# Column sums of the modulation by a product with ones, on a decoder block of one core

## The chip, the cores and the metric

The kernel runs on one core of one Trainium2 chip. The metric is the device time of one execution in microseconds (us), lower is better. TensorE (PE) multiplies, VectorE (DVE) does the elementwise work, ScalarE (ACT) activations and copies, GpSimd (POOL) and SyncE (SP) issue most of the DMAs.

## The reference

One decoder block over 512 tokens of width 2048, all in f32. A condition vector c gives six modulation vectors of 2048 each, `mod = silu(c) @ w_ada + b_ada`: shift, scale and gate of the first half, then of the second.

```
shift1, scale1, gate1, shift2, scale2, gate2 = split(mod, 6)
h = rms_norm(x, norm1_w) * (1 + scale1) + shift1
proj = h @ w_in                      # 7168 columns: attention q, k, v and recurrence q, f, i, g
attn = rms_norm(dilated_attention(q, k, v), attn_out_norm_w)
hg = rms_norm(hgrn2(...), hg_norm_w) * silu(g)
x = x + gate1 * (concat(attn, hg) @ w_out)
h2 = rms_norm(x, norm2_w) * (1 + scale2) + shift2
x = x + gate2 * (square(relu(h2 @ w_ff1)) @ w_ff2)
```

## The kernel before

**Products.** Every f32 operand of the big products is split into a rounded part (hi) and a rest (lo), and each product is three: hi hi, hi lo, lo hi. `_split` makes the two parts of the weights (whi on ScalarE, L39; wlo on VectorE, L40), with four buffers of each. So one block k (128 rows of the input width) of a group of four column blocks is 12 products of 512 moving columns, in `ch_mm` and `tok_mm` (L198 to L200, L206 to L208).

**The modulation.** It is a matrix-vector product with 100 MB of weights and runs on VectorE (`gemv`): each 128 rows of w_ada are multiplied by one number per partition and added into one of two accumulators `acc` (L127, L129). What is left is the sum over the 128 partitions, as one number per column, in a column layout: `to_cols`. It turns each 128 columns of the accumulators with a transpose on TensorE (L149), and ScalarE sums each row of the result with an accumulating copy (L152, an ACTIVATE and a read of the accumulator). For 512 columns the two accumulators are first added on VectorE (L143), so there are four transposes; for 256 columns both are turned, which is four too. Then VectorE adds the bias (L167) and, for a scale, makes (1 + scale) times norm weight (L169). `mod_cols` does this for one block of columns of one kind (kind 0 is shift1, 1 scale1, 2 gate1, 3 shift2, 4 scale2, 5 gate2), and `mod_rows` for a whole gate.

**The first stage.** The projection starts before all of the modulation is there. `first_groups` multiplies columns 4096 to 4607 and 3072 to 3327 of w_in with the normalised input scaled by scale1, block k by block k. Ahead of each pair of blocks `scale_block` finishes the sum of the 256 columns of scale1 that it needs; `scaled` then scales xnT (L332), rounds it to hi (L333) and takes the rest lo (L334). Shift1 is added later: for these columns `shift_through` multiplies shift1 itself by w_in, as a second matrix-vector product, and for all others `shifted` remakes hi and lo (L337 to L339). The second `first_groups` call takes the next 512 + 256 columns, with `shift_block` making shift1 in four blocks of 512 meanwhile.

**Order.** A scheduler places the instructions of this first part from its own estimate of their times; each engine then runs its queue strictly in order. From the projection of columns 5120 on (`hv0`) TensorE's order is the written one: the rest of the modulation (the list `later`: gate1, then scale2 and shift2 by turns, then gate2) is cut into steps by `yield`, and `project` takes 1.85 of them for each block k (2.0 in `hv0`). `tc.issue_after(ins)` places what is traced under it behind `ins` on its engine's queue.

Of the kernel before, what the change touches and what calls it, by code (L numbers as in the profile page):

```python
# [11 lines left out]
AF = mybir.ActivationFunctionType  # L12
ALU = mybir.AluOpType
AX = mybir.AxisListType

P = 128
D = 2048
S = 512
NK = D // P
# [25 lines left out]
def hybrid_block(ctx, tc, x, c, positions, norm1_w, w_ada, b_ada, w_in, q_norm_w, k_norm_w,  # L45
# [3 lines left out]
    pe, dve, act, pool = nc.tensor, nc.vector, nc.scalar, nc.gpsimd  # L49
# [18 lines left out]
    def bank(name, tag="bg"):  # L68
        return ps.tile([P, 512], F32, name=name, tag=tag)


    ident = const.tile([P, P], F32, name="ident")
    make_identity(nc, ident)
    mhalf = const.tile([P, 32], F32, name="mhalf")
    pool.memset(mhalf, -0.5)

    crow = ca.tile([P, P], F32, name="crow", tag="rows")
    nc.sync.dma_start(crow[0:NK], c[0].rearrange("(r p) -> r p", p=P))
# [4 lines left out]
    n1c = const.tile([P, NK], F32, name="n1c")  # L83
    dve.tensor_copy(n1c, ps_c[:, NK:2 * NK])
    bcol = const.tile([P, 96], F32, name="bcol")
    dve.tensor_copy(bcol, ps_c[:, 2 * NK:P])
    sc = const.tile([P, NK], F32, name="sc")
    sig_ready = act.activation(sc, ps_c[:, 0:NK], AF.Sigmoid)
    sc_ready = dve.tensor_tensor(sc, ps_c[:, 0:NK], sc, op=ALU.mult)
# [10 lines left out]
    n2c, aoc, hgc, posc = cols[:, 0:16], cols[:, 16:24], cols[:, 40:41], cols[:, 44:48]  # L100
# [15 lines left out]
    def gemv(view, vec, col0, n=512, early=False):  # L116

        accs = [(work("acc") if early else gv.tile([P, 512], F32, name="acc"))[:, 0:n] for _ in range(2)]
        nk = 512 // n
        for k0 in range(0, NK, nk):  # L120
            raw = spare.pop(0) if early and spare else slot("araw") if early else gv.tile([P, 512], F32, name="araw", bufs=4)
            raw = raw.rearrange("p (k n) -> p k n", n=n)
            nc.sync.dma_start(raw, view[:, k0:k0 + nk, col0:col0 + n])
            for k in range(k0, k0 + nk):
                acc = accs[k % 2]
                if k < 2:
                    dve.tensor_scalar(acc, raw[:, k - k0], vec[:, k:k + 1], None, op0=ALU.mult)  # L127
                else:
                    dve.scalar_tensor_tensor(acc, raw[:, k - k0], vec[:, k:k + 1], acc, op0=ALU.mult, op1=ALU.add)  # L129
            yield  # L130
        gemv.acc = accs

# [2 lines left out]
            pass  # L135
        return gemv.acc

    def to_cols(accs, dst):

        nb = accs[0].shape[1] // P  # L140
        parts = 1 if nb == 4 else 2
        if parts == 1:
            dve.tensor_tensor(accs[0], accs[0], accs[1], op=ALU.add)  # L143
        yield
        pc = bank("pc")
        for j in range(nb):
            for u in range(parts):
                c = (j * parts + u) * P
                pe.transpose(pc[:, c:c + P], accs[u][:, j * P:(j + 1) * P], ident)  # L149
        for j in range(nb):  # L150
            c = pc[:, j * parts * P:(j + 1) * parts * P]
            act.activation(c, c, AF.Copy, accum_out=dst[:, j:j + 1])  # L152

    g1c = const.tile([P, NK], F32, name="g1c")
    s1c = const.tile([P, NK], F32, name="s1c")
# [4 lines left out]
    def mod_cols(kind, b, dst, nw, n=512, early=False):  # L160

        for _ in gemv(ada_v, sc, kind * D + b * n, n, early):
            yield
        nb = n // P
        d = dst[:, b * nb:(b + 1) * nb]
        yield from to_cols(gemv.acc, d)
        dve.tensor_tensor(d, d, bcol[:, kind * NK + b * nb:kind * NK + (b + 1) * nb], op=ALU.add)  # L167
        if nw is not None:
            mod_cols.last = dve.scalar_tensor_tensor(d, d, 1.0, nw[:, b * nb:(b + 1) * nb], op0=ALU.add, op1=ALU.mult)  # L169
        yield  # L170

    def mod_rows(kind, dst):
# [53 lines left out]
    def slot(name, dt=F32):  # L226
        return io.tile([P, 512], dt, name=name, tag="io")

    def work(name, dt=F32):
        return wk.tile([P, 512], dt, name=name, tag="wk")  # L230

    def pair(i):

        return [hp.tile([P, S], F32R, name=f"{c}{i}", tag=f"{c}{i}") for c in ("hi", "lo")]
# [7 lines left out]
    hhi, hlo, spare = [], [], []  # L242
# [11 lines left out]
    for q in range(4):  # L254
        for ti in range(NT):
            jk = work("jk")
            with tc.issue_after(sc_ready.ins), tc.issue_after(sig_ready.ins):
                if q == 3 and ti % 2:
                    dve.tensor_tensor_reduce(jk, xs[ti][q], xs[ti][q], op0=ALU.mult, op1=ALU.add, scale=1.0, scalar=0.0,
                                             accum_out=ssx[:, ti, q:q + 1])  # L260
# [9 lines left out]
    xnT = []  # L270
# [36 lines left out]

    def shift_start(k0):
        if k0 == 14:
            for _ in range(12):  # L310
                bg_step()

    shift_done, behind = set(), []

# [14 lines left out]
    def scaled(k):  # L329
        for l, t in zip((hhi, hlo), pair(k)):  # L330
            l.append(t)
        act.activation(xnT[k], xnT[k], AF.Copy, scale=g1c[:, k:k + 1])  # L332
        act.copy(hhi[k], xnT[k])  # L333
        dve.tensor_tensor(hlo[k], xnT[k], hhi[k].bitcast(F32), op=ALU.subtract)  # L334

    def shifted(k):
# [6 lines left out]
    def bg_step():  # L343

        while bgw:
            try:
                return next(bgw[0])
            except StopIteration:
                bgw.pop(0)
# [198 lines left out]
    def forget(hd, src, f, bias=0.0):  # L548
        act.activation(f, src, AF.Sigmoid, bias=bias)
        dve.tensor_scalar(f, f, omlb[:, hd:hd + 1], lb[:, hd:hd + 1], op0=ALU.mult, op1=ALU.add)  # L550
# [182 lines left out]
    def keep(banks, name, scale=1.0):  # L733
        ts = []
        for b in banks:
            t = slot(name)
            act.activation(t, b, AF.Copy, scale=scale)
            ts.append(t)
        return ts

    def shift_through(col0):

        yield from gemv(win_v, s1c, col0, early=col0 < 4096 + 512)
        col = sm.tile([P, 8], F32, name="scol", bufs=2)
        yield from to_cols(gemv.acc, col[:, 0:4])
        for h in range(4):
            if col0 == 3072:
                dve.tensor_scalar(col[:, 4 + h:5 + h], col[:, h:h + 1], QS, None, op0=ALU.mult)
                sg = wk.tile([P, 512], F32, name="sg", tag="ev", bufs=2)
                act.activation(sg, hq0[h], AF.Sigmoid, scale=1.0 / QS, bias=col[:, h:h + 1])  # L750
                dve.scalar_tensor_tensor(hq0[h], hq0[h], col[:, 4 + h:5 + h], sg, op0=ALU.add, op1=ALU.mult)
            else:
                f, hd = ((f0, h), (f1, 4 + h))[(col0 - 4096) // 512]
                forget(hd, f[h], f[h], col[:, h:h + 1])
        yield

    bgw += [shift_through(4096), shift_through(3072)]
    bt, bc = first_groups(4096, 3072, scale_block, shift_start)
    f0 = keep(bt, "f")
    hq0 = keep(bc, "gq", QS)  # L760
    with tc.issue_after(mod_cols.last.ins):
        posf = ca.tile([NT, P], F32, name="posf")
        dve.tensor_copy(posf, posi)
        ps_v = bank("ps_v")
        pe.transpose(ps_v[:, 0:P], rows, ident)
        pe.transpose(ps_v[:, P:P + NT], posf, ident[0:NT, 0:NT])
        dve.tensor_copy(cols[:, 0:41], ps_v[:, 0:41])
        dve.tensor_copy(posc, ps_v[:, P:P + NT])


# [23 lines left out]
        for e in (20, 10, 0):  # L794
            u = float(2.0 ** e)
            k = rp[:, (4 + len(turns)) * 64:(5 + len(turns)) * 64]
# [26 lines left out]
    hq0 += keep(bc, "gq", QS)  # L823

    later.insert(0, shift_through(4096 + 512))

    ordered = ctx.enter_context(ExitStack())
# [552 lines left out]
```

## Time and profile before

| what | value |
|---|---|
| median of 3 runs | 2307.28 us (2306.57 to 2311.78) |
| profiled execution | 2306.17 us, its span 2304.4 us |
| mean granted TensorE clock | 0.994 |
| TensorE busy | 2230.5 us (97%) |
| VectorE busy | 1825.9 us (79%) |
| ScalarE busy | 1103.0 us (48%) |

The span is the recorded part of an execution, some 2 us shorter than its time. A busy time counts a stretch in which at least one instruction of the engine runs; products overlap, so the mean length of one product is longer than the distance from one to the next, and distances are taken from starts. A row of a timeline gives start, length, engine, line, operation, out<-in, shapes and count, and in brackets the idle time ahead and what ended it. A row of a group gives the count, then busy time and mean ns of one, then the idle time ahead. A row of waits gives the total, how many times, and the longest. In the chain of waits a row is start, length and what ran.

### The profile page before, as it was taken

To read this page: it belongs to the slowest core of one execution; us is meant where nothing else is said; L and a number is where in the kernel's file an instruction comes from. 1 tells how busy PE (TensorE), PEld (TensorE's weight loads), DVE (VectorE), ACT (ScalarE), POOL (GpSimd) and SP (SyncE) were. 2 spreads that over 40 slices of the span, in tenths; PEclk is the share of its full clock that TensorE was granted. 3 is DMA by queue.
4 is the path that set the end of the run, shared out by engine and by line. 5 is a ranking of instruction groups with operands and counts; after the bars stand their busy time and mean duration, and the time that the engine had idled before them with its cause. 6 is when DMAs were issued, how large, how long until landed. Compare 5 with 4: busy or idle time off the path is not lost.

```text
span 2304.4 us, 33163 instructions
## 1 busy us (share of the span) xinstructions
PE 2230.5 (97%) x11769; PEld 1829.2 (79%) x11769; DVE 1825.9 (79%) x2773; ACT 1103.0 (48%) x1958; POOL 458.1 (20%) x668
## 2 busy tenths in 40 slices
PE   4999999999999999999999999999998999999999
PEld 3787877888778888888887888888887888888887
DVE  6899777677776565669767988988895789967878
ACT  5555434433344553457644555565563333344332
POOL 1000022000230000001332323323232222222221
PEclk9999999999999999999999999999999999999999
DMA  9798455556545256746999799889889987999784
GB/s 327 249 337 314 123 176 156 176 162 215 178 149 182 74 186 218 259 132 220 366 382 382 252 341 355 301 297 380 310 295 369 339 288 262 364 336 335 277 302 165
DMA packets 264695, 606.71 MB, mean 263 GB/s; under 512 B 23284, under 2 KB 44032, under 8 KB 264528
## 3 DMA queue, kind: packets, MB, share of 16 engines
q1 hardware_dynamic: 186800, 332.54, 42.8%
q0 software_dynamic: 72832, 262.60, 31.1%
q10 hardware_dynamic: 4896, 9.44, 1.2%
q8 instruction: 93, 1.52, 0.3%
q14 instruction: 74, 0.61, 0.1%
HBM read 522.68 MB, written 81.81 MB: 262 GB/s over the span
## 4 chain that ended last, share of the span: by engine, by line
PE 56%; DMA 16%; DVE 14%; issue 10%; POOL 2%; ACT 1%; SPq 0%; DVEq 0%; POOLq 0%; ACTq 0%
PE f L1160 9%; PE f L1161 9%; PE f L1159 9%; DMA araw<-in_w_ada_dram 7%; PE prj L198 4%; PE prj L200 4%; PE prj L199 4%; DMA f_lod<-fs 3%; DVE acc L129 3%; PE f L208 2%; PE f L206 2%; PE f L207 2%; DVE vlo L1146 2%; DVE wlo L40 2%; PE prj L206 2%
## 5 line engine op out<-in xcount | busy, mean ns | idle before, releaser
L1145 ACT CAST vhi<-raw 128x1024 fp32r<-128x1024 f32 x392 | 412.8, 1055 | 547.1 <-PE f L1161 434.3
L1146 DVE TENSOR_TENSOR vlo<-raw,vhi 128x1024 fp32r<-128x1024 f32 x392 | 477.4, 1225 | 154.3 <-ACT vhi L1145 153.5
L1159 PE MATMUL f<-vhi,Fh 128*128 128x512 f32 x1376 | 537.6, 391 | 8.3 <-DMA Fh<-h_hid 3.6
L1160 PE MATMUL f<-vlo,Fh 128*128 128x512 f32 x1376 | 538.1, 391 | 3.0 <-DVE vlo L1146 3.0
L1161 PE MATMUL f<-vhi,Fl 128*128 128x512 f32 x1376 | 537.2, 390 | 2.1 <-DMA Fl<-f_lod 1.3
L39 ACT CAST whi<-wraw 128x512 fp32r<-128x512 f32 (+1 forms) x368 | 219.8, 601 | 449.3 <-PE prj L200 323.7
L198 PE MATMUL prj<-whi,hi 128*128 128x512 f32 x896 | 365.0, 407 | 1.3 <-ACT gg L698 1.3
L200 PE MATMUL prj<-whi,lo 128*128 128x512 f32 x896 | 351.5, 392 | 0.0
L199 PE MATMUL prj<-wlo,hi 128*128 128x512 f32 x896 | 350.8, 391 | 0.0
L40 DVE TENSOR_TENSOR wlo<-wraw,whi 128x512 fp32r<-128x512 f32 (+1 forms) x368 | 245.1, 670 | 111.7 <-ACT whi L39 107.1
L129 DVE SCALAR_TENSOR_TENSOR acc<-araw,sc,acc 128x512 f32<-128x512 f32 (+1 forms) x392 | 253.9, 678 | 98.5 <-DMA araw<-in_w_ada_dram 97.2
L1159 PEld LDWEIGHTS f<-vhi,Fh 128*128 128x128 f32 x1376 | 259.0, 188 | 63.3 <-issue 7.1
L1160 PEld LDWEIGHTS f<-vlo,Fh 128*128 128x128 f32 x1376 | 259.0, 188 | 61.7 <-DVE vlo L1146 8.3
L1161 PEld LDWEIGHTS f<-vhi,Fl 128*128 128x128 f32 x1376 | 259.1, 188 | 56.7 <-DMA Fl<-f_lod 1.8
L1129 DVE TENSOR_TENSOR raw<-raw,raw 128x1024 f32<-128x1024 f32 x224 | 269.5, 1223 | 1.8 <-DMA raw<-in_w_ff_dram 1.5
L198 PEld LDWEIGHTS prj<-whi,hi 128*128 128x128 f32 x896 | 169.4, 189 | 36.5 <-ACT gg L698 1.6
L200 PEld LDWEIGHTS prj<-whi,lo 128*128 128x128 f32 x896 | 168.9, 188 | 36.8
L199 PEld LDWEIGHTS prj<-wlo,hi 128*128 128x128 f32 x896 | 169.6, 189 | 32.4 <-DVE wlo L40 0.4
L1097 POOL DMA_DIRECT2D Fh<-f_hid x112 | 80.9, 722 | 428.3 <-PE f L1161 414.8
L208 PE MATMUL f<-hi,wlo 128*128 128x512 f32 x256 | 99.8, 390 | 0.6 <-DVE wlo L40 0.6
L206 PE MATMUL f<-hi,whi 128*128 128x512 f32 x256 | 100.2, 391 | 0.0
L207 PE MATMUL f<-lo,whi 128*128 128x512 f32 x256 | 99.6, 389 | 0.0
(306 smaller groups left out, 2956.9 us busy)
## 6 DMA issues: line engine op xcount, KB each, us to landing
raw<-in_w_ff_dram SPq DMA_DIRECT2D x224, 512.0 KB, 10.0
araw<-in_w_ada_dram SPq DMA_DIRECT2D x384, 256.0 KB, 4.3
Fh<-f_hid POOLq DMA_DIRECT2D x112, 512.0 KB, 6.5
Fl<-f_lod POOLq DMA_DIRECT2D x112, 512.0 KB, 7.4
wraw<-in_w_in_dram SPq DMA_DIRECT2D x104, 512.0 KB, 4.1
Fh<-h_hid POOLq DMA_DIRECT2D x60, 512.0 KB, 6.8
Fl<-h_lod POOLq DMA_DIRECT2D x60, 512.0 KB, 8.3
f_hid<-part POOLq DMA_DIRECT2D x48, 512.0 KB, 8.1
```

The costliest lines, as they stand in the source:

```text
L39: nc.scalar.copy(hi, src)
L40: (eng or nc.vector).tensor_tensor(lo, src, hi.bitcast(F32), op=ALU.subtract)
L129: dve.scalar_tensor_tensor(acc, raw[:, k - k0], vec[:, k:k + 1], acc, op0=ALU.mult, op1=ALU.add)
L198: pe.matmul(banks[ti], lhsT=hi[:, ts], rhs=whi, start=first, stop=False)
L199: pe.matmul(banks[ti], lhsT=hi[:, ts], rhs=wlo, start=False, stop=False)
L200: pe.matmul(banks[ti], lhsT=lo[:, ts], rhs=whi, start=False, stop=last)
L1129: dve.tensor_tensor(dst, a, b, op=ALU.subtract)
L1145: act.copy(hi, src)
L1146: split_done.append(dve.tensor_tensor(lo, src, hi.bitcast(F32), op=ALU.subtract))
L1159: pe.matmul(banks[t], lhsT=fh[u][:, a, ts], rhs=whi[:, a], start=first, stop=False)
L1160: pe.matmul(banks[t], lhsT=fh[u][:, a, ts], rhs=wlo[:, a], start=False, stop=False)
L1161: pe.matmul(banks[t], lhsT=fl[u][:, a, ts], rhs=whi[:, a], start=False, stop=end)
```

## The change

The transposes and the accumulating copies go. `col_sums` multiplies each 128 columns of an accumulator, as the weights of a product, by one column of ones; the two accumulators of a sum are added up in PSUM. For 512 columns that is eight products with one moving column, for 256 four. The sum of the two accumulators on VectorE (L143) goes too. For a scale, ScalarE then makes each column of (1 + scale) times norm weight straight from PSUM with an Identity activation, with the norm weight as scale and a bias that `scale_bias` has once made for all columns, (1 + b) times norm weight. For the other kinds one VectorE addition of the bias reads PSUM.

Three edits of order come with it. `scaled` makes the rounded part hi first, and the scaled xnT after it. The twelve first steps of the shift sums are placed behind the last instruction of the scale sums (`shift_start`). And the sums of `shift_through` are issued five steps behind their matrix-vector product, not one.

```diff
-    pool.memset(mhalf, -0.5)
+    pool.memset(mhalf[:, 0:16], -0.5)
+    pool.memset(mhalf[:, 16:32], 1.0)
+    ones = mhalf[:, 16:17]
...
+    def scale_bias(kind, nw):
+        b = bcol[:, kind * NK:(kind + 1) * NK]
+        return dve.scalar_tensor_tensor(b, b, 1.0, nw, op0=ALU.add, op1=ALU.mult)
+    scale_bias(1, n1c)
...
-    def to_cols(accs, dst):
-        nb = accs[0].shape[1] // P
-        parts = 1 if nb == 4 else 2
-        if parts == 1:
-            dve.tensor_tensor(accs[0], accs[0], accs[1], op=ALU.add)
-        yield
-        pc = bank("pc")
-        for j in range(nb):
-            for u in range(parts):
-                c = (j * parts + u) * P
-                pe.transpose(pc[:, c:c + P], accs[u][:, j * P:(j + 1) * P], ident)
-        for j in range(nb):
-            c = pc[:, j * parts * P:(j + 1) * parts * P]
-            act.activation(c, c, AF.Copy, accum_out=dst[:, j:j + 1])
+    def col_sums(accs, lag=1, tag="bg"):
+        for _ in range(lag):
+            yield
+        pc = bank("pc", tag=tag)
+        for j in range(accs[0].shape[1] // P):
+            for u in range(2):
+                pe.matmul(pc[:, j:j + 1], lhsT=accs[u][:, j * P:(j + 1) * P], rhs=ones, start=u == 0, stop=u == 1)
+        return pc
+    def to_cols(accs, dst, lag=1, tag="bg"):
+        pc = yield from col_sums(accs, lag, tag)
+        act.copy(dst, pc[:, 0:dst.shape[1]])
...
-        yield from to_cols(gemv.acc, d)
-        dve.tensor_tensor(d, d, bcol[...], op=ALU.add)
-        if nw is not None:
-            mod_cols.last = dve.scalar_tensor_tensor(d, d, 1.0, nw[...], op0=ALU.add, op1=ALU.mult)
+        pc = yield from col_sums(gemv.acc)
+        if nw is None:
+            dve.tensor_tensor(dst[...], pc[:, 0:nb], bcol[...], op=ALU.add)
+        else:
+            for j in range(nb):
+                k = b * nb + j
+                mod_cols.last = act.activation(dst[:, k:k + 1], pc[:, j:j + 1], AF.Identity, scale=nw[:, k:k + 1],
+                                               bias=bcol[:, kind * NK + k:kind * NK + k + 1])
+            mod_cols.last_dve = gemv.last
...
     def shift_start(k0):
         if k0 == 14:
-            for _ in range(12):
-                bg_step()
+            with tc.issue_after(mod_cols.last_dve.ins):
+                for _ in range(12):
+                    bg_step()
...
+        act.activation(hhi[k], xnT[k], AF.Copy, scale=g1c[:, k:k + 1])
         act.activation(xnT[k], xnT[k], AF.Copy, scale=g1c[:, k:k + 1])
-        act.copy(hhi[k], xnT[k])
...
-        yield from to_cols(gemv.acc, col[:, 0:4])
+        yield from to_cols(gemv.acc, col[:, 0:4], 5)
```

The lines of the changed kernel are numbered anew: L129 is L138 there, L149 is L155, L332 and L333 are L347 and L346, L198 to L200 are L211 to L213, L206 to L208 are L219 to L221.

ScalarE's queue at the first two blocks k, before:

```order
L282 COPY xnT<-ptx 128x512 x2
L332 ACTIVATE xnT<-xnT,g1c 128x512
L282 COPY xnT<-ptx 128x512
L332 ACTIVATE xnT<-xnT,g1c 128x512
L282 COPY xnT<-ptx 128x512
L39 CAST whi<-wraw 128x512 x2
L333 CAST hi_473<-xnT 128x512
```

And now:

```order
L295 COPY xnT<-ptx 128x512 x2
L346 ACTIVATE hi_471<-xnT,g1c 128x512
L295 COPY xnT<-ptx 128x512
L346 ACTIVATE hi_476<-xnT,g1c 128x512
L295 COPY xnT<-ptx 128x512
L39 CAST whi<-wraw 128x512 x2
L347 ACTIVATE xnT<-xnT,g1c 128x512
```

The rounded parts of both blocks stand ahead of the two weight casts, where the scaling of xnT stood.

VectorE's queue at the last three scale sums (128x256 are scale sums, 128x512 shift sums), before:

```order
L129 SCALAR_TENSOR_TENSOR acc<-araw,sc,acc 128x512
L129 SCALAR_TENSOR_TENSOR acc<-araw,sc,acc 128x256
L129 SCALAR_TENSOR_TENSOR acc<-araw,sc,acc 128x512
L169 SCALAR_TENSOR_TENSOR g1c<-g1c,n1c 128x2
L40 TENSOR_TENSOR wlo<-wraw,whi 128x256
L129 SCALAR_TENSOR_TENSOR acc<-araw,sc,acc 128x256
L167 TENSOR_TENSOR g1c<-g1c,bcol 128x2
L129 SCALAR_TENSOR_TENSOR acc<-araw,sc,acc 128x512
L129 SCALAR_TENSOR_TENSOR acc<-araw,sc,acc 128x256
```

And now:

```order
L138 SCALAR_TENSOR_TENSOR acc<-araw,sc,acc 128x256 x3
L348 TENSOR_TENSOR lo_999<-xnT,hi_998 128x512
L348 TENSOR_TENSOR lo_1004<-xnT,hi_1003 128x512
L40 TENSOR_TENSOR wlo<-wraw,whi 128x256 x2
L138 SCALAR_TENSOR_TENSOR acc<-araw,sc,acc 128x256 x6
L136 TENSOR_SCALAR acc<-araw,sc 128x512 x2
```

The first shift sum (L136 on 128x512) stands behind the last of the scale sums, and the g1c instructions are gone from this queue.

TensorE's queue at the sums of the fourth block of shift1, before (in the products of `hv0`, its 13th product group):

```order
L199 MATMUL prj<-wlo,hi_579 128x512
L200 MATMUL prj<-whi,lo_580 128x512
L149 MATMUL pc<-ident,acc 128x128 x4
L198 MATMUL prj<-whi,hi_579 128x512
L199 MATMUL prj<-wlo,hi_579 128x512
```

And now (in the second `first_groups` call, ahead of its block k = 14):

```order
L220 MATMUL prc<-lo_1111,whi 128x512
L221 MATMUL prc<-hi_1110,wlo 128x512
L155 MATMUL pc<-mhalf,acc 128x1 x8
L219 MATMUL prj<-hi_1171,whi 128x512
L220 MATMUL prj<-lo_1172,whi 128x512
```

Eight products with the ones (a column of mhalf) stand where four transposes stood, and 75 products earlier in the queue.

More of the change, by code (lines that the diff above doesn't have):

```diff
@@ L128, in gemv @@
                 else:
-                    dve.scalar_tensor_tensor(acc, raw[:, k - k0], vec[:, k:k + 1], acc, op0=ALU.mult, op1=ALU.add)
+                    gemv.last = dve.scalar_tensor_tensor(acc, raw[:, k - k0], vec[:, k:k + 1], acc, op0=ALU.mult,
+                                                         op1=ALU.add)
             yield
@@ L164, in mod_cols @@
         nb = n // P
-        d = dst[:, b * nb:(b + 1) * nb]
-        yield from to_cols(gemv.acc, d)
-        dve.tensor_tensor(d, d, bcol[:, kind * NK + b * nb:kind * NK + (b + 1) * nb], op=ALU.add)
-        if nw is not None:
-            mod_cols.last = dve.scalar_tensor_tensor(d, d, 1.0, nw[:, b * nb:(b + 1) * nb], op0=ALU.add, op1=ALU.mult)
+        pc = yield from col_sums(gemv.acc)
+        if nw is None:
+            dve.tensor_tensor(dst[:, b * nb:(b + 1) * nb], pc[:, 0:nb],
+                              bcol[:, kind * NK + b * nb:kind * NK + (b + 1) * nb], op=ALU.add)
+        else:
[4 more added lines that the diff above has]
+            mod_cols.last_dve = gemv.last
         yield
@@ L760, in hybrid_block @@
     hq0 = keep(bc, "gq", QS)
-    with tc.issue_after(mod_cols.last.ins):
+    with tc.issue_after(mod_cols.last.ins), tc.issue_after(mod_cols.last_dve.ins):
         posf = ca.tile([NT, P], F32, name="posf")
@@ L767, in hybrid_block @@
         dve.tensor_copy(cols[:, 0:41], ps_v[:, 0:41])
+        scale_bias(4, n2c)
         dve.tensor_copy(posc, ps_v[:, P:P + NT])
```

## The prediction

> **What bounds the kernel now.** I read the page's busy times first, then busy time by stretch, then TensorE's waits, then the timelines around each wait.
>
> ```profile
> span 2304.4 us, 33163 instructions
> PE 2230.5 (97%) x11769; PEld 1829.2 (79%) x11769; DVE 1825.9 (79%) x2773; ACT 1103.0 (48%) x1958; POOL 458.1 (20%) x668
> 0.00:240.00 240.00, 199.44 (x877) 162.27 (x878) 206.32 (x454) 127.20 (x289) 14.93 (x33) 0.96 0.88 300
> 240.00:1070.00 830.00, 814.80 (x5470) 663.67 (x5469) 601.71 (x1258) 387.80 (x1006) 82.64 (x127) 1.00 0.54 170
> 1070.00:2304.00 1234.00, 1216.24 (x5426) 1003.28 (x5424) 1017.84 (x1063) 587.96 (x665) 360.50 (x508) 1.00 0.87 319
> ```
>
> The first column after the bounds is the stretch, then come TensorE's busy time, its weight loads, VectorE, ScalarE, GpSimd, clock, DMA share and GB/s. TensorE bounds everything. It idles 40.6 us in the first 240 us, only 15.2 us in the 830 us after (the rest of the modulation's work lies there), and 17.8 us in the last 1234 us, which the change doesn't touch. So time is to be won ahead of 240 us, and what is added to TensorE behind it is paid nearly in full. The 40.6 us:
>
> ```profile
> PE ptx L280 <- ACT xs L274: 12.7, 1, 12.7
> PE prj L206 <- ACT hi L333: 6.9, 4, 4.1
> PE pc L149 <- DVE acc L143: 4.9, 1, 4.9
> ```
>
> The 12.7 us and what precedes them wait for x, which the change leaves alone. The other two rows are its targets. Their places, and the clock behind them:
>
> ```profile
> 37.06 1.19 PE L206 MATMUL prj<-hi,whi 128*128 128x512 f32 x4 [0.68 <-ACT hi L333]
> 52.75 2.02 PE L206 MATMUL prj<-hi,whi 128*128 128x512 f32 x4 [1.97 <-ACT hi L333]
> 58.58 1.07 PE L206 MATMUL prj<-hi,whi 128*128 128x512 f32 x4
> 94.46 2.07 PE L206 MATMUL prj<-hi,whi 128*128 128x512 f32 x4 [4.05 <-ACT hi L333]
> 101.66 1.07 PE L206 MATMUL prj<-hi,whi 128*128 128x512 f32 x4
> 105.75 0.27 PE L149 MATMUL pc<-ident,acc 128*128 128x128 f32 x1
> 214.98 1.12 PE L149 MATMUL pc<-ident,acc 128*128 128x128 f32 x4 [4.86 <-DVE acc L143]
> 215.75 0.78 PE L198 MATMUL prj<-whi,hi 128*128 128x512 f32 x1
> 220.59 0.40 PE L198 MATMUL prj<-whi,hi 128*128 128x512 f32 x1
> ```
>
> One row block k takes 18 products (4 + 2 column blocks, three each). Undisturbed that is 101.66 to 105.75, 4.09 us or 0.227 us a product. Behind the wait at 52.75 the same 18 take 5.83 us (to 58.58), behind the one at 94.46 7.20 us (to 101.66), and behind 214.98 twelve products take 4.84 us instead of 2.73. So each wait costs a second time, through the slow clock after it: 1.7, 3.1 and 2.1 us.
>
> **The change part by part.** First, the way from a finished scale sum to TensorE. For the block that stopped TensorE at 94.46:
>
> ```profile
> 85.32 0.49 PE L149 MATMUL pc<-ident,acc 128*128 128x128 f32 x3
> 85.84 0.37 ACT L152 ACTIVATE pc<-pc 128x256 f32<-128x256 f32 x1 [0.62 <-PE pc L149]
> 88.84 0.17 DVE L167 TENSOR_TENSOR g1c<-g1c,bcol 128x2 f32<-128x2 f32 x1
> 92.36 0.17 DVE L169 SCALAR_TENSOR_TENSOR g1c<-g1c,n1c 128x2 f32<-128x2 f32 x1
> 92.57 1.33 ACT L332 ACTIVATE xnT<-xnT,g1c 128x512 f32<-128x512 f32 x2 [1.14 <-DVE g1c L169]
> 93.81 1.12 ACT L333 CAST hi<-xnT 128x512 fp32r<-128x512 f32 x2
> 60.00:80.00 20.00, 19.78 (x92) 16.10 (x91) 20.00 (x53) 10.70 (x25) 0.00 (x0) 1.00 1.09 354
> 80.00:100.00 20.00, 15.65 (x60) 11.73 (x59) 20.00 (x48) 9.09 (x21) 0.00 (x0) 0.84 0.77 262
> 100.00:120.00 20.00, 20.00 (x90) 16.26 (x89) 13.56 (x46) 10.10 (x21) 0.00 (x0) 0.98 0.29 80
> ```
>
> From the product at 85.32 to the rounded part at 93.81 pass 8.5 us, though the rows between them hold 2.0 us of work: the two tiny VectorE instructions stand in the queue of an engine busy 20.00 of 20 us. After the change ScalarE does it alone: two instructions on one column each, at most the 0.37 us of the row at 85.84, then at once the rounded part, whose scaled xnT comes behind it. That is about 1.5 us and no VectorE. The wait at 94.46 and the one at 52.75 should go. ScalarE has room (about 10 of 20 us), so its added work costs nothing; if it had none, 0.7 us a block would show. The first rounded part moves ahead of two weight casts, which gives most of the 0.68 us at 37.06. Of 6.9 us of waits I take 4.9 as gained and leave 2.0, since the sums themselves come at the pace of a full VectorE; with 1.7 + 3.1 of clock that is **-9.7 us**.
>
> The shift sums queued behind, the second edit, help here:
>
> ```profile
> L129 DVE SCALAR_TENSOR_TENSOR acc<-araw,sc,acc 128x512 f32<-128x512 f32 x10 | 7.7, 769 | 0.0
> L143 DVE TENSOR_TENSOR acc<-acc 128x512 f32<-128x512 f32 x7 | 5.0, 715 | 0.0
> ```
>
> Ten shift sums, 7.7 us, stood between the last scale sums. Now they wait for the last of them; behind them are queued later shift sums, and TensorE's first shift product waits for those. VectorE's idle 6.4 us at 100 to 120 us take most of the ten, so no term. The DMAs that feed them keep their place in SP's queue, behind the same w_in loads. The L143 sums go, 5.0 us of VectorE up to 235 us; that is under a busy TensorE, and serves as slack.
>
> At 214.98 TensorE waited for a sum of the f columns' shift, whose product is now issued four steps later (two blocks k in the projection, 5.4 us of products), and the 4.86 + 2.1 us go: **-7.0 us**.
>
> Now what TensorE pays. A transpose is one record; an f32 product is two. The ten products of one head in L498 are 20 records, each with its own weight load; so the 8 products of 512 columns are 16 records where 4 stood, and the 4 of a scale block 8. No row shows a product with one moving column. The nearest rows, from the chain (first two), from the groups, and the timeline (last):
>
> ```profile
> 440.26 2.23 PE po L498 x20
> 1700.86 1.75 PE pt L1189 x16
> L498 PEld LDWEIGHTS po<-av,p_sb 128*128 128x128 f32 x160 | 19.1, 192 | 0.6
> L651 PEld LDWEIGHTS pC<-z 128*64 128x64 f32 x64 | 4.3, 137 | 2.9 <-issue 1.1 <-DVE z L598 0.4 <-DVE f L605 0.4
> L571 PEld LDWEIGHTS pA<-z 128*32 128x32 f32 x768 | 8.8, 110 | 5.6 <-issue 5.3 <-DVE Sx L604 0.4
> L149 PE MATMUL pc<-ident,acc 128*128 128x128 f32 x76 | 11.6, 274 | 0.3 <-ACT p_sb L489 0.3
> 252.00 0.46 PE L571 MATMUL pA<-z 128*32 128x32 f32 x32
> ```
>
> A record of L498 (same weights, 128 moving columns) takes 2.23/20 = 0.111 us, a transpose 1.75/16 = 0.109. Weight loads of 128, 64 and 32 columns last 192, 137 and 110 ns: 0.85 ns for each column, so 109 ns of the 192 grow with the weights, and one moving column in place of 128 can't shorten them. I take 0.111. The ends are 0.192 (loads that don't overlap at all) and 0.46/32 = 0.014 (L571's 32-column weights, if loads bound nothing). At 0.111 a 512-column sum takes 16 x 0.111 = 1.78 us against 4 x 0.109 = 0.44, **+1.34**; a scale block 0.89 against 0.44, +0.45.
>
> The Trainium skill (TensorE: Matmul & The Clock Gate, section LDWEIGHTS (loading the stationary operand)) says the same against this change: a load's time goes by its weight columns, P/1.2 ns, an estimate of 107 ns for 128. The slope above agrees. By it the sum would be 2 us lower.
>
> Seven scale blocks on the path: 7 x 0.45 = **+3.2**. Five 512-column sums from 120 to 240 us: **+6.7**. Behind 240 us stand 76/4 = 19 of them: 19 x 1.34 = **+25.5**. Some of the 15.2 us of idle there will take them up:
>
> ```profile
> PE pC L645 <- DVE z L598: 4.2, 2, 3.1
> PE ptq L451 <- ACT p_sb L489: 2.4, 2, 1.7
> ```
>
> These wait for VectorE and ScalarE, which a slower TensorE and fewer tiny instructions give time; a third of the idle, **-5.0**. The accumulating reads of ScalarE and the tiny VectorE sums that go lie under TensorE there: 0. The split memset and the bias scaled once for all columns: two or three instructions of some 0.17 us under waits for DMA, 0.
>
> Sum: -9.7 - 7.0 + 3.2 + 6.7 + 25.5 - 5.0 = +13.7 us on the profiled execution's 2306.17, so **2320 us**; its runs' median is 2307.28, 1.1 us higher, within what I can tell.
>
> **The rivals.** *The loads are cheap* (faster). With p us a record the sum is -16.7 - 5.0 - 3.1 - 10.6 + 440 p: it turns at p = 0.080. If a load took half of a transpose's 0.109 us, its stream the other half, p = 0.055 gives -11 us: 2295. At the end of 0.014 it is -29, 2277. For it: L571's records; against it: the slope of the loads. The same page of the Trainium skill, section Back-to-back issue gap, gives an issue floor of 25 ns for 1 to 64 moving columns; by that alone, an estimate, the time would be 2282. No run here shows it for 128 weight columns. Chance 0.27.
>
> *The wait moves* (slower). TensorE's product for the fourth shift block now stands in the second column group, some 17 us of products (75 of 0.227) earlier than before, and needs all 64 shift sums. If VectorE is late there by 5 us, TensorE stops, and with 3 us of slow clock the time is 2328. For it: VectorE was full at 60 to 100 us; against it: it loses 5.0 us of L143 and its idle stretch. It decides from about 2 us late. Chance 0.12.
>
> *The loads don't overlap*: p = 0.19 gives +48 us: 2354. Against it: L498's records follow each other at 0.111 with loads of 192 ns. Chance 0.07.
>
> *It cancels*: p near 0.08, or much more of the idle taken up: within 4.6 us. Chance 0.11.
>
> **How the numbers follow.** The forecast (p from 0.095 to 0.125, 2313 to 2326 and some us of the other terms: 2309 to 2330) has 0.43. Slower by over 0.2% (4.6 us, about what a measurement of this kernel tells from no change) are forecast, moved wait and no overlap, 0.62 less 0.02 at the forecast's edge; faster are the cheap loads, 0.27 less 0.02; the same is what is left, 0.11 + 0.04. The range leaves out one in ten on each side: up past the moved wait to 2336, down into the cheap loads to 2293.
>
> **What would show it.** Right: the records of the new products 0.10 to 0.12 us apart and 16 to a sum; no wait for hi at 50 to 95 us; no wait at 210 us; the second column group ending 6 us or so earlier than now; TensorE's busy time up by some 30 us, most of it behind 240 us. Wrong: records 0.06 us apart or fewer of them; a new wait of TensorE for VectorE's sums between 110 and 190 us; more than half of the late idle gone.

## The result and the profile after

The changed kernel takes 2329.36 us in the median (2327.82 to 2333.70 in four runs) against 2308.98 us before (2306.57 to 2311.78): a ratio of 1.0091, 95% interval 1.0072 to 1.0110, so slower by 20.4 us. The forecast was slower, 2320 us, with a range of 2293 to 2336 us; direction and range held, the rise was half as large again as forecast. The profiled execution of the changed kernel took 2333.7 us, the longest of the four, so its trace shows some 4 us more than the usual run. All ratios below are to the kernel before on the same chip, and leave one disturbed run out (9674.65 us, in the first experiment).

The page's first lines after:

```profile
span 2331.6 us, 33602 instructions
PE 2267.9 (97%) x12089; PEld 1869.5 (80%) x12089; DVE 1810.4 (78%) x2727; ACT 1076.2 (46%) x1770; POOL 452.2 (19%) x669
```

Busy time by the same three stretches as before (TensorE, its weight loads, VectorE, ScalarE, GpSimd, clock, DMA share, GB/s):

```profile
0.00:240.00 240.00, 207.81 (x996) 174.55 (x997) 201.37 (x433) 122.45 (x241) 14.64 (x34) 0.99 0.88 300
240.00:1070.00 830.00, 815.33 (x5538) 668.07 (x5537) 564.40 (x1190) 339.03 (x822) 76.99 (x127) 0.99 0.52 165
1070.00:2331.00 1261.00, 1244.73 (x5558) 1026.91 (x5556) 1044.66 (x1107) 614.68 (x710) 360.56 (x508) 1.00 0.86 315
```

TensorE is busy 37.4 us longer (2267.9 against 2230.5). Ahead of 240 us it idles 32.2 us instead of 40.6. From 240 to 1070 us it idles 14.7 us, as before (15.2), though it does more.

Three markers say where the time was lost. These are rows for single lines of the program: count, shortest/median/longest in ns, and the first and last start in us. First the kernel before, then the changed one: the second column group's products (L206, L219), the first heads' products (L571, L585), and the projections (L198, L211):

```profile
L206 PE MATMUL prc<-hi,whi x64: 387/389/632, 47.3 to 189.5; 128*128 128x512 f32 x64
L571 PE MATMUL pA<-gq,kk x256: 196/196/217, 248.4 to 656.1; 128*32 128x32 f32 x128
L198 PE MATMUL prj<-whi,hi x896: 387/389/796, 188.2 to 1011.3; 128*128 128x512 f32 x180
```

```profile
L219 PE MATMUL prc<-hi,whi x64: 387/389/486, 47.8 to 187.0; 128*128 128x512 f32 x64
L585 PE MATMUL pA<-gq,kk x256: 196/196/217, 247.1 to 674.0; 128*32 128x32 f32 x128
L211 PE MATMUL prj<-whi,hi x896: 387/389/796, 187.9 to 1039.0; 128*128 128x512 f32 x180
```

At the end of the second column group the changed kernel is 2.5 us ahead (187.0, 189.5), at the first heads 1.3 us (247.1, 248.4), and at the last projection product 27.7 us behind (1039.0, 1011.3). From there to the end nothing more is lost (the spans differ by 27.2). So the loss lies between 247 and 1039 us.

TensorE's waits after (us in total, times, longest), from three stretches: up to 190 us (first row), 190 to 260 us (second), 260 to 1045 us:

```profile
PE prj L219 <- ACT hi L346: 0.5, 1, 0.5
PE pc L155 <- DVE acc L138: 2.9, 2, 2.7
PE pC L665 <- DVE z L612: 3.5, 1, 3.5
PE ptq L465 <- ACT p_sb L503: 3.4, 2, 2.1
PE pC L659 <- DVE z L612: 2.5, 3, 1.1
PE prj L212 <- DVE wlo L40: 1.6, 1, 1.6
```

The 6.9 us for the rounded parts are 0.5. The 4.9 us for a shift sum are 2.9, at another sum. The waits for VectorE's z and for p_sb are still there.

One late sum, and the sum that waits (timeline of TensorE; the number after x counts records):

```profile
517.61 1.84 PE L155 MATMUL pc<-mhalf,acc 128*128 128x1 f32 x16
519.31 0.49 PE L211 MATMUL prj<-whi,hi 128*128 128x512 f32 x1
519.64 0.40 PE L212 MATMUL prj<-wlo,hi 128*128 128x512 f32 x1
...
236.07 0.35 PE L155 MATMUL pc<-mhalf,acc 128*128 128x1 f32 x2 [2.67 <-DVE acc L138]
236.64 3.00 PE L155 MATMUL pc<-mhalf,acc 128*128 128x1 f32 x14 [0.22 <-DVE acc L138]
239.51 0.77 PE L211 MATMUL prj<-whi,hi 128*128 128x512 f32 x1
240.08 0.63 PE L212 MATMUL prj<-wlo,hi 128*128 128x512 f32 x1
```

The 16 records take 1.70 us to the next product's start (519.31 - 517.61), 0.106 us each. The first product behind them takes 0.33 us to the next one instead of 0.23. With that, a sum of 512 columns costs TensorE 1.83 us wherever neither a wait nor a slow clock is near (median of the 19 late ones, by the time until 12 or 14 products later, less 0.2275 us for each of these). The same reading of the kernel before gives 0.47 us for four transposes. The difference is 1.36 us.

### The profile page after: what moved, and what is told of

The parts are those of the page before. It is cut to its first block, busy times and chain, and to the rows that moved or that the text cites. A ratio compares the mean times of both kernels' runs of the same rounds, so it can differ in the third digit from the quotient of the medians.

```text
span 2331.6 us, 33602 instructions
## 1 busy us (share of the span) xinstructions
PE 2267.9 (97%) x12089; PEld 1869.5 (80%) x12089; DVE 1810.4 (78%) x2727; ACT 1076.2 (46%) x1770; POOL 452.2 (19%) x669
## 4 chain that ended last, share of the span: by engine, by line
PE 74%; DMA 9%; DVE 7%; issue 6%; ACT 2%; POOL 2%; SPq 0%; ACTq 0%; DVEq 0%; POOLq 0%
PE f L1176 11%; PE f L1175 11%; PE f L1174 11%; PE prj L211 8%; PE prj L213 8%; PE prj L212 8%; DMA araw<-in_w_ada_dram 3%; DMA Fl<-h_lod 2%; PE pc L155 2%; PE f L221 2%; PE f L219 2%; PE f L220 2%; DMA Fl<-f_lod 2%; PE prj L219 2%; PE prj L221 2%
## 5 line engine op out<-in xcount | busy, mean ns | idle before, releaser
L40 DVE TENSOR_TENSOR wlo<-wraw,whi 128x512 fp32r<-128x512 f32 (+1 forms) x368 | 244.3, 667 | 184.2 <-ACT whi L39 180.0
L211 PE MATMUL prj<-whi,hi 128*128 128x512 f32 x896 | 367.1, 410 | 1.3 <-ACT gg L712 1.3
L213 PE MATMUL prj<-whi,lo 128*128 128x512 f32 x896 | 354.0, 395 | 0.0
L138 DVE SCALAR_TENSOR_TENSOR acc<-araw,sc,acc 128x512 f32<-128x512 f32 (+1 forms) x392 | 249.9, 672 | 69.4 <-DMA araw<-in_w_ada_dram 69.0
L213 PEld LDWEIGHTS prj<-whi,lo 128*128 128x128 f32 x896 | 170.4, 190 | 37.4
L211 PEld LDWEIGHTS prj<-whi,hi 128*128 128x128 f32 x896 | 170.6, 190 | 36.7 <-ACT gg L712 1.6
L219 PE MATMUL f<-hi,whi 128*128 128x512 f32 x256 | 100.2, 391 | 0.0
L221 PE MATMUL f<-hi,wlo 128*128 128x512 f32 x256 | 99.8, 390 | 0.3 <-DVE wlo L40 0.3
```

Of the source, the lines that this page charges most:

```text
L40: (eng or nc.vector).tensor_tensor(lo, src, hi.bitcast(F32), op=ALU.subtract)
L138: gemv.last = dve.scalar_tensor_tensor(acc, raw[:, k - k0], vec[:, k:k + 1], acc, op0=ALU.mult, op1=ALU.add)
L211: pe.matmul(banks[ti], lhsT=hi[:, ts], rhs=whi, start=first, stop=False)
L213: pe.matmul(banks[ti], lhsT=lo[:, ts], rhs=whi, start=False, stop=last)
```

## The experiments

**Transposes back for the large sums.**

```diff
     def to_cols(accs, dst, lag=1, tag="bg"):
-        pc = yield from col_sums(accs, lag, tag)
-        act.copy(dst, pc[:, 0:dst.shape[1]])
+        dve.tensor_tensor(accs[0], accs[0], accs[1], op=ALU.add)
...
+            pe.transpose(pc[:, j * P:(j + 1) * P], accs[0][:, j * P:(j + 1) * P], ident)
...
+            act.activation(c, c, AF.Copy, accum_out=dst[:, j:j + 1])
```

> The changed kernel, but the 24 sums over 512 columns are made as before: VectorE adds the two halves, four transposes, ScalarE's accumulating copies. Products with the ones are left only in the eight scale blocks; the order edits stay. Theory (the ones-products behind the first column groups are the loss, about 1.34 us of TensorE for each 512-column sum, 24 of them): 32 us below the changed kernel's 2329, so 2297 (2292 to 2302), which is 10 us or so under the kernel before. Rival (the products' price is small, and the loss comes of the order edits, a wait that moved or work that VectorE and ScalarE lost their place for): 2318 to 2330.

Measured: 2312.33 us, ratio 1.0018 (1.0004 to 1.0031). That is 0.7%, some 17 us, below the changed kernel, about half of the theory's 32 and more than the rival's 11 at most. TensorE's busy time did fall as the theory has it, by 35.9 us to 2232.0. So the products' price is right, but by the medians only half of it comes back as time. By the two profiled executions it is 26.3 us (spans of 2305.3 and 2331.6), since this one is 5.3 us under its kernel's median and the changed kernel's 4.3 us over. Part of what is missing are waits for VectorE's z: 11.8 us between 240 and 1045 us, 6.5 in the changed kernel. In this trace the second column group ends at 183.0 us, 6.5 ahead of the kernel before, the heads start at 244.2, only 4.2 ahead, and by the last projection product (1009.7 against 1011.3) 1.6 us are left. The profiled execution is the second shortest of this kernel's runs, so the usual one keeps less still.

**Half the products.** VectorE adds the halves, then four products:

```diff
+        if parts == 1:
+            dve.tensor_tensor(accs[0], accs[0], accs[1], op=ALU.add)
...
-            for u in range(2):
+            for u in range(parts):
```

> The changed kernel, but VectorE adds the two halves of each 512-column sum first, so that four products with the ones (8 records) stand where eight (16 records) stood. Theory (each record costs its 0.106 us of TensorE): 24 x 8 x 0.106 = 20 us less, 2309 (2304 to 2313), whatever VectorE pays for 24 additions of 0.7 us under TensorE. Rival (a sum costs by the break it makes in TensorE's stream, its wait and its slow start, not by its records): under 6 us less, 2323 or more.

Measured: 2319.72 us, ratio 1.0060 (1.0039 to 1.0081), 7 us or so below the changed kernel: between theory and rival. A late sum costs what the theory says:

```profile
506.61 0.94 PE L159 MATMUL pc<-mhalf,acc 128*128 128x1 f32 x8
507.42 0.49 PE L215 MATMUL prj<-whi,hi 128*128 128x512 f32 x1
```

8 records, 0.81 us to the next product, 0.94 with the slower product behind. Its waits for z between 240 and 1045 us come to 15.0 us, against 6.5 in the changed kernel: VectorE's 24 additions of 0.70 us are not free there. By the traces TensorE is busy 25.3 us less and the span only 16.4 us shorter, so these waits take nearly all that is missing.

**One accumulator.** All row blocks are added into one tile, which halves the products and needs no addition:

```diff
-                acc = accs[k % 2]
-                if k < 2:
+                acc = accs[0]
+                if k < 1:
```

> The changed kernel with one accumulator for each sum instead of two (even and odd row blocks added into the same tile): no addition of halves, and half the products in all sums, scale blocks too. Theory (records alone count): 24 x 8 x 0.106 + 7 x 4 x 0.106 = 23 us less, 2306 (2301 to 2311). Rival (each VectorE instruction that reads what the one before it wrote takes longer, say 0.06 us of 0.67): VectorE, full from 60 to 100 us, gets 10 us or so later there, the waits for the rounded part come back, 2312 to 2320.

Measured: 2306.61 us, ratio 1.0000 (0.9990 to 1.0010). The theory's time, and its count of records. Half of the rival came too: waits for hi (3.1 us) and lo (2.7 us) are back in the first group. But not for the rival's reason, since the dependent instructions take 751 ns as against 749; why they are back isn't shown. The waits for z are 3.0 us.

**Half as many weight columns for each product.** Twice as many products:

```diff
+                for h in (0, 64):
+                    pe.matmul(pc[h:h + 64, j:j + 1], lhsT=accs[u][:, j * P + h:j * P + h + 64], rhs=ones, ...
```

> The changed kernel with every product with the ones cut in two, 64 weight columns each: 32 records for a 512-column sum instead of 16, each loading half as many columns. Theory (a record's price is its weight load, which goes by the columns): records some 0.055 us apart, a sum still 1.7 us, the time within 5 us of the changed kernel's 2329. Rival (a price for each record, whatever it loads): records 0.10 us apart, a sum 3.4 us, the time 2329 + 440 x 0.106 = 2376.

Measured: 2323.54 us in a single run. The rival falls. The theory is too dear as well, for a sum of 32 records now takes 1.16 us, not 1.7:

```profile
507.68 1.10 PE L156 MATMUL pc<-mhalf,acc 128*64 128x1 f32 x32
508.71 0.50 PE L212 MATMUL prj<-whi,hi 128*128 128x512 f32 x1
```

1.03 us to the next product, 0.032 a record: half the columns cost less than a third.

**One accumulator and transposes.** The first experiment with one accumulator for each 512-column sum.

```diff
-    dve.tensor_tensor(accs[0], accs[0], accs[1], op=ALU.add)
+    if len(accs) == 2:
+        dve.tensor_tensor(accs[0], accs[0], accs[1], op=ALU.add)
```

> The first experiment's kernel (products with the ones in the scale blocks alone, four transposes for each 512-column sum), with one accumulator for each 512-column sum, so that VectorE's 23 additions of halves, 0.70 us each, go. Theory (the first experiment won 6.5 us by 183 us and lost them again between 430 and 765 us, since TensorE then waited for VectorE's z; with 16 us of work taken from VectorE it keeps them): z waits at or under the 7.6 us of the kernel before, 2298 (2294 to 2302). Rival (the early gain is lost to something else than VectorE's work, the positions of the sums or the loads): 2304 to 2309, z waits 10 us or more.

Measured: 2303.87 us, ratio 0.9992 (0.9981 to 1.0003). The waits for z fall to 2.3 us, as the theory says, but the time doesn't follow. The gain is lost earlier, in TensorE's waits between 190 and 260 us:

```profile
PE pc L165 <- DVE acc L138: 15.0, 2, 8.3
```

The row of the heads' first products in the same kernel:

```profile
L598 PE MATMUL pA<-gq,kk x256: 196/196/217, 254.6 to 656.5; 128*32 128x32 f32 x128
```

TensorE waits 15.0 us for two shift sums (8.3 and 6.7 us), and the heads start 6.2 us later than in the kernel before. The rival had the time (2304 to 2309) nearly right and looked for the loss outside VectorE's z, but it forecast waits for z of 10 us or more; neither text named these two waits. Why this kernel's products for the later shift sums start 6 to 15 us later than the next experiment's (205.5 against 192.6 us for the fourth block of shift1, 246.9 against 232.3 for the last one before the heads), which has the same accumulators, isn't settled.

**A quarter of the weight columns, one accumulator.**

```diff
+                for h in range(0, P, 32):
+                    pe.matmul(pc[h:h + 32, j:j + 1], lhsT=accs[u][:, j * P + h:j * P + h + 32], rhs=ones, ...
```

> The changed kernel with one accumulator for each 512-column sum and every product with the ones cut in four, 32 weight columns each: 32 records for a 512-column sum. Theory (a record's price is its weight load; 32-column records follow each other at 0.014 us in L571's rows): a sum costs 0.45 to 0.65 us of TensorE, as much as four transposes (0.47), a scale block the same (0.92 before), and with VectorE relieved the time is 2297 (2292 to 2302). Rival (the 64-column records took 1.16/32 = 0.036 us, and below that a price for each record stands): a sum still costs 1.1 us or more, 2308 to 2313.

Measured: 2290.51 us, ratio 0.9933 (0.9920 to 0.9947). The theory's price holds, the time is 1.5 us under its range, and this beats both kernels:

```profile
494.77 0.43 PE L156 MATMUL pc<-mhalf,acc 128*32 128x1 f32 x32
495.14 0.50 PE L213 MATMUL prj<-whi,hi 128*128 128x512 f32 x1
```

32 records in 0.37 us, 0.0116 a record, and 0.49 us with the slower product behind: what four transposes cost (0.47), without ScalarE's accumulating copies and without VectorE's additions. A scale block's 32 records cost the same in place of 0.92. The widths were changed together with the place in the array, so a smaller load and loads that run side by side are not told apart here. The Trainium skill ("TensorEngine Tiling (Array Packing)", section Key Properties) says that different tiles can load and multiply in parallel; the less than proportional prices, 0.106, 0.032 and 0.0116 us for 128, 64 and 32 columns, agree with that.

**The later issue undone.** The product for a sum of `shift_through` is issued one step after it, not five (the expectations call this the fifth edit); one single run, then seven.

```diff
-        yield from to_cols(gemv.acc, col[:, 0:4], 5)
+        yield from to_cols(gemv.acc, col[:, 0:4])
```

> The changed kernel with the fifth edit undone alone: the product for a sum of the f columns' shift is issued one step after the sum, not five. Theory (the later issue is what took the wait at 214.98 away, and the wait of 2.7 us at 236 is the one for the next sum): a wait of TensorE for the sum of 4 to 6 us at 205 to 220 us, and none or a small one at 236; the pA products start 3 us or so later than the changed kernel's 247.1. Rival (the wait had moved rather than gone: VectorE's pace decides when these sums are ready, whatever the place of their product): the waits between 200 and 245 us come to the same 3 us or so in total, within 1.5, and pA starts within 1.5 us of 247.1.

> The kernel of the seventh experiment again (the changed kernel, the fifth edit undone alone), now timed. Its one look gave 2313.9 against the changed kernel's 2329. Theory (the four added steps hold back what stands behind them in the background: the last two loads of the next shift stand in SP's queue behind five weight loads that wait for buffers, 229.8 us in place of 208.1, and every later sum comes four steps later, where TensorE then waits for z): 12 to 18 us under the changed kernel, 2312 to 2317, a ratio of 1.002 to 1.004 to the kernel before. Rival (one look of a kernel that varies by some us): within 5 us of 2329, ratio 1.007 or more.

Measured: 2313.91 us in the single run, 2319.27 us in the median of the seven, ratio 1.0050 (1.0032 to 1.0068), an interval that stands clear of the changed kernel's. So 0.4%, 9.5 us, of the slowdown are this edit's: less than the theory's 12 to 18, more than the rival's 5. Both expectations for the single run fell, the theory's with the wrong sign: there is no wait for a sum at all between 190 and 260 us, neither at the early place nor at 236. The heads start 5 us earlier than in the changed kernel (row of L585 in the trace of the second measurement):

```profile
L585 PE MATMUL pA<-gq,kk x256: 196/196/217, 241.8 to 661.2; 128*32 128x32 f32 x128
```

The middle stretch of the same trace has 8.4 us of TensorE's idle time instead of 14.7:

```profile
240.00:1070.00 830.00, 821.64 (x5588) 674.21 (x5586) 578.26 (x1207) 350.74 (x842) 80.77 (x127) 0.99 0.52 167
```

And its only wait for z up to 1045 us is this one, where the changed kernel has 6.5 us:

```profile
PE pC L659 <- DVE z L612: 0.7, 1, 0.7
```

The reason for the wait at 236 stands in SP's queue. First the changed kernel (start, us, DMA issues):

```profile
208.37 0.33 SPq L132 DMA_DIRECT2D araw<-in_w_in_dram  x1
209.03 0.33 SPq L132 DMA_DIRECT2D araw<-in_w_ada_dram  x1
209.75 19.99 SPq L202 DMA_DIRECT2D wraw<-in_w_in_dram  x5
229.79 0.94 SPq L132 DMA_DIRECT2D araw<-in_w_in_dram  x2
```

The same queue with the edit undone:

```profile
209.55 2.98 SPq L132 DMA_DIRECT2D araw<-in_w_in_dram  x3
212.84 0.33 SPq L132 DMA_DIRECT2D araw<-in_w_ada_dram  x1
213.56 23.28 SPq L202 DMA_DIRECT2D wraw<-in_w_in_dram  x6
```

The jobs in the background run one after the other. Four more steps of one job hold back the next one's loads by four steps, and its last two then stand behind five weight loads that are issued only as buffers come free, from 209.75 to 229.74. They land at 233.8 and 234.4 us; VectorE's last two additions run at 235.18, right behind a weight split (L40) that stands ahead of them in its queue, and TensorE's product waits for them.

**The queueing of the shift sums undone.**

```diff
-            with tc.issue_after(mod_cols.last_dve.ins):
-                for _ in range(12):
-                    bg_step()
+            for _ in range(12):
+                bg_step()
```

> The changed kernel with the order edit undone alone that queues the shift sums behind the last scale sum. Theory (the waits for the rounded part went by taking the tiny VectorE instructions off the path; the queueing adds a little): one wait for hi of 1 to 3 us at 80 to 100 us, the second column group ends 1 to 4 us later than the changed kernel's 187.9. Rival (the queueing is what keeps the last scale sums early): waits of 4 us or more at 85 to 100 us with slow products behind them, the second column group ends 6 us or more later. A third way (the queueing does nothing or harms): no such wait, the group ends no later than 188.

Measured: 2333.23 us in a single run. The last scale sum's product starts at 105.4 us instead of 97.5, yet TensorE waits only 1.0 us for hi and 0.9 for lo up to 190 us, and the second column group ends 1.4 us later. The theory's small help, though without its single wait of 1 to 3 us.

**The first experiment with the later issue undone too.** The two diffs above together.

> The first experiment's kernel (transposes and VectorE's additions for the 512-column sums, products with the ones in the scale blocks alone) with the fifth edit undone too. Theory (the fifth edit took back what the first column group had won): no load of the next shift behind blocked weight loads, z waits of 8 us or less, 12 us or so under that kernel's 2312, 2299 (2294 to 2303). Rival (VectorE, with its additions, bounds the stretch from 200 to 430 us whatever the steps; then the earlier product waits for its sum as in the kernel before): waits for the sums of 5 us or more between 200 and 240 us, 2304 to 2312.

Measured: 2305.25 us, ratio 0.9998 (0.9983 to 1.0012): the rival. The second column group ends 5.9 us ahead of the kernel before (183.6 against 189.5), and more than half of the lead is lost at once: the product that waited at 214.98 us in the kernel before starts 2.3 us earlier here (212.69). TensorE's timeline from 184 us:

```profile
184.74 0.66 PE L164 MATMUL pc<-ident,acc 128*128 128x128 f32 x4
187.15 0.50 PE L224 MATMUL prj<-wlo,hi 128*128 128x512 f32 x1 [1.75 <-DVE wlo L40]
...
188.57 0.63 PE L223 MATMUL prj<-whi,hi 128*128 128x512 f32 x1
```

Busy time in the next 20 us (columns as above):

```profile
190.00:200.00 10.00, 10.00 (x42) 8.18 (x41) 9.80 (x16) 6.71 (x12) 0.00 (x0) 0.92 1.04 384
200.00:210.00 10.00, 7.88 (x35) 6.19 (x33) 10.00 (x19) 2.25 (x4) 0.00 (x0) 1.00 1.05 387
```

And TensorE's only wait between 190 and 260 us:

```profile
PE pc L164 <- DVE acc L159: 4.8, 1, 4.8
```

TensorE arrives before its weights do (1.75 us and slow products behind them), then waits 4.8 us for the first sum that VectorE has to add up. VectorE is busy 9.8 and 10.0 of 10 us there and the DMA share is 1.04 and 1.05, so both are full, and part of what TensorE wins ahead of this stretch is given back in it. Not all: the heads still start 3.4 us ahead of the kernel before (245.0, 248.4), and in the sixth experiment, without the additions, a second group that ends 9.4 us earlier (180.1) leaves the heads 7.9 us ahead (240.5). Where the additions of L159 are gone and the product stands at the same early place (the kernel with only the later issue undone), it starts at 208.09 us without a wait, in this kernel at 212.69 after one. So the later product was not needed to take the wait at 214.98 away. The additions' going fits: six of them, 4.2 us in all, stand in VectorE's queue up to this sum, which is done at 212.63 us here and by 208.09 there. The order of VectorE's queue changed with them, and its part isn't separated.

**The quarter loads with the later issue undone, and with its lag kept but the next job moved on meanwhile.** The first has the diff shown above; the second:

```diff
-                return next(bgw[0])
+                late = next(bgw[0])
...
+            if late and len(bgw) > 1:
+                next(bgw[1])
```

> The sixth experiment's kernel (one accumulator, 32 weight columns a product) with the fifth edit undone. Theory (the five-step lag costs it the waits of 1.3 and 5.3 us at 207 and 232 us and the slow products behind them, 2.2 us): 2282 (2277 to 2286). Rival (TensorE is 7 us earlier there than in the changed kernel, so that the sums are late by VectorE's pace and the loads' anyway, and the product that stands four steps earlier waits the longer): waits of 6 us or more between 195 and 240 us, 2287 to 2295.

> The sixth experiment's kernel with the five steps kept for the product, but with the next job in the background moved on during four of them, so that its loads and VectorE instructions no longer stand behind the lag. Theory (late product and early loads together): no wait above 3 us between 195 and 240 us, 2281 (2276 to 2286), at or under the kernel with the lag undone. Rival (VectorE's pace alone, or the two jobs side by side on VectorE delay the first sum): 2287 to 2295.

Measured: 2289.57 us, ratio 0.9925 (0.9905 to 0.9946), and 2288.50 us, ratio 0.9923 (0.9904 to 0.9942). Both times are the rivals', and neither differs from the sixth experiment's 0.9933. TensorE's waits for shift sums between 190 and 260 us remain, in the first kernel:

```profile
PE pc L156 <- DVE acc L138: 6.1, 1, 6.1
```

and in the second:

```profile
PE pc L156 <- DVE acc L138: 5.2, 2, 3.9
```

With TensorE 6 us ahead of the changed kernel at the end of the second group (181.0 against 187.0), the sum comes no sooner than with the later issue undone alone (207.59 us in the first kernel, 208.09 at the latest there), so part of the lead is waited away, as in the experiment before. All three are about 0.7% faster than the kernel before, 1.6% faster than the changed one. So the later issue, which costs 9.5 us in the changed kernel, costs nothing that can be told here, and in the pair with transposes about 0.2% (1.0018 against 0.9998, with intervals that overlap).

## Why the prediction was right, and where it was not

- **The first column group (-9.7 us).** Right. The group pair ends 2.5 us earlier although it holds seven dearer scale blocks (forecast 3.2) and four large sums at 1.83 us where three stood at 0.47 (5.9), so the waits and the clock behind them gave 2.5 + 3.2 + 5.9 = 11.6 us. The queueing of the shift sums had no term, and a single run without it moved the group's end by 1.4 us.
- **The wait at 214.98 (-7.0 us).** This step failed. The credit was given to the later issue of the product; the wait is gone without it, most likely by the additions of L143 going. The later issue brought a wait of its own, 2.7 us at 236, with the slow products behind it 6.3 us in all. Between the second group and the first heads two sums at 1.83 us stand where three stood at 0.47, 2.2 us more, so 4.8 of the 7.0 should have been left as a gain; 1.2 were lost (leads of 2.5 and 1.3). What was missed is that a step added to a job moves the DMAs of the job behind it: SP's queue was weighed for the queueing of the shift sums, not for this edit.
- **The price of a record (0.111 us).** Right: 0.106 in a run of 16, 1.36 us more for a sum where 1.34 were forecast, 16 records each. The number that decided the sign came from a row with 128 moving columns, and holds with one.
- **The idle time taken up (-5.0 us).** Failed in this kernel: 14.7 us of idle from 240 to 1070 us, against 15.2. With the later issue undone it is 8.4 us, so 6.8 us are taken up there, as forecast for a slower TensorE. The edit puts every later sum four steps on (the first behind 240 us starts at 282.68 us instead of 269.62), and the waits for z are back; that their new places make them is what the traces suggest, no run moved the places alone. The two other pairs that differ in this edit agree: 11.8 us of waits for z against 6.9 with transposes (first and tenth experiment), 5.8 against 1.9 with quarter loads.
- **The sum.** Without the two failed terms the forecast is +25.7 us; the trace shows +27.2, the medians +20.4. In the trace the stretch from the first heads to the last projection product is 29.0 us longer: the sums' own records are 22.9 of it, and the same 2661 projection products take 6.3 us more (635.5 against 629.2, idle time left out), partly the slower product behind each sum and partly slow stretches such as the one at 390 us shown below, for which the forecast had no term. Both failures go back to one edit, which cost about 10 us and was booked as a gain. The forecast's +13.7 is near what the kernel without this edit came to (+12.6 by the medians, 2319.27 against 2306.70). That the changed kernel still lies in the range is owed to the range's 43 us, not to these two terms.
- **The rivals.** The cheap loads didn't come at 128 weight columns. At 32 they do, and then go below the floor of 25 ns that the Trainium skill gives (TensorE: Matmul & The Clock Gate, section Back-to-back issue gap): 11.6 ns a record. The wait moved, but to the last shift product at 236, not to the fourth block of shift1 in the second column group, which at 177.87 waits for nothing. Loads without overlap didn't come.
- **What would show it.** Records 0.106 us apart and 16 to a sum, no wait for hi from 50 to 95 us beyond one of 0.5, none at 210: as listed. The second column group's end was listed as 6 us earlier and is 2.5, since the list forgot the sums' own price inside it. Busy time rose by 37.4 us, not 30.

## What to carry to other kernels

A product with one moving column cost here what its weights cost: look for a row with the same number of weight columns, count records and not products, and try narrower weights, placed side by side, before anything else. A delay added in a chain of background jobs delays the loads of the job behind it; look where these then stand in SP's queue, and what blocks that queue. Before booking time won early, read VectorE's and the DMA's share in the stretch that it leads into: where both are at 1.0, part of it was given back here.

## What the runs showed of the hardware that was not expected

The clock fell once in the changed kernel's trace behind a sum that nothing had waited for:

```profile
388.38 1.95 PE L155 MATMUL pc<-mhalf,acc 128*128 128x1 f32 x16
390.19 0.57 PE L211 MATMUL prj<-whi,hi 128*128 128x512 f32 x1
390.56 0.63 PE L212 MATMUL prj<-wlo,hi 128*128 128x512 f32 x1
...
393.92 0.39 PE L211 MATMUL prj<-whi,hi 128*128 128x512 f32 x1
```

From 390.19 to 393.92 nine products take 3.73 us instead of 2.05, though TensorE is busy without a break from 360 to 400 us; the granted clock is 0.57 from 390 to 394. The sum stands behind 32 short products of a head (0.38 us). In the single run without the later issue two sums that nothing waited for (555.60 and 637.75 us) have the same slow stretch behind them (1.7 us each), and both come right behind a head's short products, too. But short records alone don't bring it: in the changed kernel three more sums stand right behind a head's products (331.34, 579.13 and 661.43 us) without it, and in the second measurement without the later issue the later one of those two sums (641.66 us there) has none. What the clock fell for stays open. The other surprise is the price by width: 0.106, 0.032 and 0.0116 us a record for 128, 64 and 32 weight columns.
